# Two transformer blocks in split float32: seven held chunks with operand quarters between them, later head steps, and feed-forward pairs on one three-bank tag

## The chip, the cores and the metric

The kernel runs on one core of one Trainium2 chip. What is measured is the time of one execution on the device, in microseconds (us). A run of the program takes about 1.9 ms. The engines that matter are TensorE (PE in the profile; its weight loads are PEld), VectorE (DVE), ScalarE (ACT), GpSimd (POOL) and SyncE (SP), which issues the DMAs. PE writes its results to PSUM, which has eight banks of 512 float32 columns per partition.

## The reference

Two transformer blocks run one after the other on 256 tokens of width 2048, all in float32.

```python
# block 1
h = rms_norm(x, norm_g); proj = h @ w_in                      # 2048 -> 8192
ya = stick_breaking_attention(qa, ka, va); yb = chunk_band_attention(qb, kb, vb, ...)
x = x + concat(ya * silu(ga), yb * silu(gb)) @ w_out
# block 2
mod = silu(c) @ w_ada + b_ada                                 # 2048 -> 12288, six vectors
h = rms_norm_2(x, g_pre_mix) * (1 + sc1) + sh1; z = h @ w_in
o_a = mla_branch(cq, ckv, kr, ...)     # 16 heads, causal softmax
o_b = swa_branch(qs, ks, vs, ...)      # 32 heads of 64, window 128, a sink per head
mix = (sigmoid(za) * o_a + sigmoid(zb) * o_b) @ w_o
x = x + gt1 * rms_norm_2(mix, g_post_mix)
h = rms_norm_2(x, g_pre_ffn) * (1 + sc2) + sh2
u = causal_dwconv(h @ w_up)                                   # 2048 -> 2 x 5632, width 3
y = (silu(u[:, :5632]) * u[:, 5632:]) @ w_down
x = x + gt2 * rms_norm_2(y, g_post_ffn)
```

The 256 tokens are two token blocks of 128, which are called block 0 and block 1 of tokens below.

## The kernel before, in words

**Products.** A float32 product is made of three passes with each operand split into a high and a low part: `hi*hi + hi*lo + lo*hi`. In the projections the weight is stationary and the 256 tokens stream (256 columns, L270 to L272); in `wide` the first two passes share one matmul of 512 columns (L277) and the third has 256 (L278). Where an output row per token is wanted (`xmm`), 128 tokens are stationary and 256 or 512 weight columns stream (L293 to L295).

**The stream of weights.** `Stream` brings all weights in chunks of 128 x 1024 floats (512 KB): SP issues the DMA into one of five raw buffers, ACT writes the high part (`whi`, L123), DVE the low part (`wlo`, L125), and PE uses the two parts in the order in which the chunks were listed. Split chunks wait in slots. There are four (`AHEAD` is 3), and nine where a chunk was listed with `S.more` set (`AHEAD + 1 + MORE`). A slot is free when PE has used the chunk for the last time. Where PE keeps chunks for a second use, `S.base` stops the count, so that held chunks take slots which the chunks ahead would else have. `S.gate` puts a split behind a named instruction on ACT and DVE.

**Heads.** A head is a generator that the stream moves on by ticks, two for each chunk, which is 24 matmuls. Its softmax does DVE work on the scores, waits `DL[0]` ticks, does the exponentials on ACT, waits `DL[1]`, normalizes on POOL (`e`, L443, behind a reciprocal on DVE, L439), waits `DL[2]`, puts three transposes on PE (`t`, L450) which ACT copies to `pT`, waits `DL[3]`, and then `attend` puts three matmuls on PE (`o`, L457, L458). `DS` is the table of the 32 window heads, `DM` that of the 16 latent heads. On PE and SP instructions run in the order in which the code makes them; on ACT, DVE and POOL a scheduler orders them.

**The output projection and its end.** `mix @ w_o` goes in four column groups of 512, c = 0 to 3, of eight chunks each (`x_group`). Group 3 (tag `s`) handles the two token blocks apart: block 0 of tokens in every chunk, block 1 of tokens for the last `HOLD` = 4 chunks only after all of block 0. So `o_last(0)`, which closes block 0 of tokens (norm, residual `xs`, norm again, diagonal `dg`), runs beside the held matmuls. `operand(b, q)` makes a quarter of the feed-forward operand of token block b: four products with the diagonal on PE (`t`, L1390), scale and shift into `ht` on ACT and DVE, high part `h` on ACT, low part on DVE (L1400). `first_up` runs the first eight feed-forward chunks, again block 0 of tokens first (12 matmuls a chunk), with further `operand` calls between, then block 1 of tokens. `turn` brings its results over and starts the convolutions.

**Feed-forward pairs.** `up_pair(i)` fills two PSUM banks of two chunks each, the first of tag `g` (three banks) and the second of tag `s` (two); `post` reads a bank with ACT (`z`), DVE (L1556) and the convolution `conv` (L1511, L1513).

## Time and profile before

| | |
|---|---|
| median of three runs | 1911.71 us (1911.47 to 1912.13) |
| profiled execution | 1911.32 us |
| its span in the trace | 1909.5 us |
| PE busy | 1886.9 us (99%) |
| PEld, DVE, ACT, POOL busy | 1708.7, 1361.9, 1015.8, 193.0 us |
| chain of waits | PE 93%, DVE 2%, ACT 2%, issue 1%, DMA 1%, POOL 1% |
| HBM read | 434.73 MB, 229 GB/s over the span |

Busy times are sums over an engine's instructions; PE's ends are modelled. The span is what the trace covers, and the 1.8 us between it and the execution's time lie outside of it. PEclk in the profile is the share of full speed that TensorE's clock was granted. An instruction's idle time stands in brackets behind it with what ended it.

### The profile page before, as it was taken

Reading aid. Unit: us, or ns where it says so; the run is one execution under the profiler, and the core shown is the slowest. Engines: PE = TensorE matmul, PEld = TensorE weight load, DVE = VectorE, ACT = ScalarE, POOL = GpSimd, SP = SyncE. Lnnn points to the kernel's source line nnn. Section 1 sums busy time; section 2 is a strip of 40 time slices with the busy share of each in tenths; the row PEclk is TensorE's granted clock in tenths of the full one; section 3 lists DMA queues with packets and bytes.
Section 4 is the critical chain, followed back from the end, with each engine's and each line's share of the span. In section 5 each row is a group of like instructions: output and inputs, shape, how many; then the busy total and the mean of one; then the engine's idle time right before and its main releaser. Section 6 shows DMA issues by size and latency. Waiting matters only on the chain.

```text
span 1909.5 us, 31900 instructions
## 1 busy us (share of the span) xinstructions
PE 1886.9 (99%) x12148; PEld 1708.7 (89%) x12148; DVE 1361.9 (71%) x2211; ACT 1015.8 (53%) x1642; POOL 193.0 (10%) x298
## 2 busy tenths in 40 slices
PE   9999999999999999999999999999999999999998
PEld 9988889999999999999998878888888888888886
DVE  7777867767787777777877765888888777644444
ACT  7445454445555555554666556555555555543442
POOL 0001020001223323330123000000000000000000
PEclk9999999999999999999999999999999999999999
DMA  9888777757597877768655764777777665656564
GB/s 366 297 285 293 243 269 258 239 188 250 194 327 239 268 259 264 258 215 268 195 167 189 232 210 142 244 236 247 241 246 242 189 187 188 187 181 188 189 191 124
DMA packets 128169, 438.92 MB, mean 230 GB/s; under 512 B 14352, under 2 KB 20368, under 8 KB 127760
## 3 DMA queue, kind: packets, MB, share of 16 engines
q1 hardware_dynamic: 127872, 436.88, 69.6%
q8 instruction: 95, 1.56, 0.3%
q14 instruction: 58, 0.48, 0.1%
q10 hardware_dynamic: 144, 0.01, 0.0%
HBM read 434.73 MB, written 2.10 MB: 229 GB/s over the span
## 4 chain that ended last, share of the span: by engine, by line
PE 93%; DVE 2%; ACT 2%; issue 1%; DMA 1%; POOL 1%; SPq 0%; DVEq 0%; POOLq 0%; ACTq 0%
PE g L270 11%; PE g L271 11%; PE g L272 11%; PE s L277 8%; PE g L277 8%; PE g L293 7%; PE g L295 7%; PE g L294 7%; PE s L278 4%; PE g L278 4%; PE s L293 3%; PE s L294 3%; PE s L295 3%; PE o L457 1%; PE t L450 1%
## 5 line engine op out<-in xcount | busy, mean ns | idle before, releaser
L125 DVE TENSOR_TENSOR wlo<-raw,whi 128x1024 fp32r<-128x1024 f32 (+2 forms) x623 | 764.2, 1228 | 394.4 <-ACT whi L123 390.4
L123 ACT ACTIVATE whi<-raw 128x1024 fp32r<-128x1024 f32 (+2 forms) x623 | 652.0, 1048 | 631.5 <-PE g L271 136.8
L270 PE MATMUL g<-h,whi 128*128 128x256 f32 x880 | 253.6, 288 | 0.0
L272 PE MATMUL g<-h,wlo 128*128 128x256 f32 x880 | 247.8, 282 | 0.0
L271 PE MATMUL g<-h,whi 128*128 128x256 f32 x880 | 247.7, 281 | 0.0
L277 PE MATMUL s<-h,whi 128*128 128x512 f32 x672 | 240.7, 399 | 3.8 <-DVE u L1513 3.8
L392 DVE SCALAR_TENSOR_TENSOR raw<-raw,crep 128x1024 f32<-128x1024 f32 x192 | 240.7, 1254 | 2.1 <-DMA raw<-in_ada_dram 1.7
L277 PE MATMUL g<-h,whi 128*128 128x512 f32 x672 | 239.2, 397 | 0.0
L278 PE MATMUL s<-h,wlo 128*128 128x256 f32 x672 | 189.9, 283 | 0.0
L278 PE MATMUL g<-h,wlo 128*128 128x256 f32 x672 | 189.1, 281 | 0.0
L271 PEld LDWEIGHTS g<-h,whi 128*128 128x128 f32 x880 | 166.6, 189 | 0.0
L270 PEld LDWEIGHTS g<-h,whi 128*128 128x128 f32 x880 | 166.6, 189 | 0.0
L272 PEld LDWEIGHTS g<-h,wlo 128*128 128x128 f32 x880 | 166.3, 189 | 0.0
L277 PEld LDWEIGHTS s<-h,whi 128*128 128x128 f32 x672 | 126.9, 189 | 35.5 <-issue 4.0
L277 PEld LDWEIGHTS g<-h,whi 128*128 128x128 f32 x672 | 126.1, 188 | 31.1
L270 PE MATMUL g<-hx,whi 128*128 128x256 f32 x448 | 127.7, 285 | 0.0
L278 PEld LDWEIGHTS s<-h,wlo 128*128 128x128 f32 x672 | 127.4, 190 | 0.0
L278 PEld LDWEIGHTS g<-h,wlo 128*128 128x128 f32 x672 | 126.7, 188 | 0.0
L272 PE MATMUL g<-hx,wlo 128*128 128x256 f32 x448 | 125.8, 281 | 0.0
L271 PE MATMUL g<-hx,whi 128*128 128x256 f32 x448 | 125.8, 281 | 0.0
L293 PE MATMUL g<-whi,hx 128*128 128x512 f32 x256 | 104.6, 409 | 0.0
L295 PE MATMUL g<-whi,hx 128*128 128x512 f32 x256 | 101.0, 395 | 0.0
(351 smaller groups left out, 3872.3 us busy)
## 6 DMA issues: line engine op xcount, KB each, us to landing
raw<-in_ada_dram SPq DMA_DIRECT2D x192, 512.0 KB, 4.3
raw<-in_wup_dram SPq DMA_DIRECT2D x176, 512.0 KB, 4.3
raw<-in_w_dram SPq DMA_DIRECT2D x127, 512.0 KB, 4.8
raw<-in_wz_dram SPq DMA_DIRECT2D x122, 512.0 KB, 4.6
raw<-in_wdn_dram SPq DMA_DIRECT2D x88, 512.0 KB, 3.5
raw<-in_wo_dram SPq DMA_DIRECT2D x64, 512.0 KB, 4.4
raw<-in_wuq_dram SPq DMA_DIRECT2D x24, 384.0 KB, 3.5
raw<-in_wuv_dram SPq DMA_DIRECT2D x8, 512.0 KB, 4.5
```

The costliest lines, as they stand in the source:

```text
L123: nc.scalar.activation(out=hi[:, :n], in_=raw, func=AF.Copy)
L125: last = nc.vector.tensor_tensor(out=lo[:, :n], in0=raw, in1=hi[:, :n].bitcast(F32), op=ALU.subtract)
L270: mm(out, lhsT=whi, rhs=ahi, start=first, stop=False)
L271: mm(out, lhsT=whi, rhs=alo, start=False, stop=False)
L272: mm(out, lhsT=wlo, rhs=ahi, start=False, stop=last)
L277: mm(two(out), lhsT=whi, rhs=both, start=first, stop=False)
L278: mm(out[:, :T], lhsT=wlo, rhs=ahi, start=False, stop=last)
L293: mm(out, lhsT=ahi[:, t], rhs=hi[:, w], start=first, stop=False)
L294: mm(out, lhsT=ahi[:, t], rhs=lo[:, w], start=False, stop=False)
L295: mm(out, lhsT=alo[:, t], rhs=hi[:, w], start=False, stop=last)
L392: stt(out=raw, in0=raw, scalar=1.0, in1=crep_now[0][:, h * 1024:(h + 1) * 1024], op0=ALU.mult, op1=ALU.mult, accum_out=modh[:, k:k + 1])
L450: nc.tensor.transpose(pt[:, j * P:(j + 1) * P], e[:, j * P:(j + 1) * P], ident)
```

## The change

Four edits, with a constant or a list each for the first two.

- **The first window head** (h = 0) has its own table `DS0`, in which the transposes come two ticks later.
- **The latent heads** get `DM = (2,1,3,3)` instead of `(2,1,2,2)`: transposes one tick later, `attend` one more. Two more chunks of `o_second` stand before the chunk with `o_start`, which ends the last heads.
- **The end of the output projection** holds seven chunks instead of four. `mid` puts the operand quarters (0,0) and (0,1) behind the fifth of the seven held chunks; the four idle matmuls (`WARM`) go. `o_last(1)` makes residual and diagonal of token block 1 itself. `operand` works in two halves of two tiles, so that a quarter's high and low part are two instructions each. Operand (1,2) moves ahead of `out_z`, (1,3) to behind the second block.
- **Feed-forward pairs** take both of their banks from tag `g`.

```diff
-COLD, WARM = 24, 4
+COLD = 24
-    DS = (2,2,2,3)
-    DM = (2,1,2,2)
+    DS0, DS = (2,2,4,3), (2,2,2,3)
+    DM = (2,1,3,3)
...
-    def x_group(srcs, acts, handler, tot, width, tag="g", apart=None, listed=True):
+    def x_group(srcs, acts, handler, tot, width, tag="g", apart=None, listed=True, hold=HOLD, mid=None):
...
-                if apart is not None and c >= nch - HOLD:
+                if apart is not None and c >= nch - hold:
                     S.base = 1 << 30 if c == nch - 1 else min(S.base, S.nrun)
...
                 if c == nch - 1:
                     r.append(lambda: apart(0, box["b"][0]))
-                    r += [lambda j=j, d=d: one(box[d], d, j, 1) for d in range(c - HOLD + 1, c + 1) for j in js]
+                    for n, d in enumerate(range(c - hold + 1, c + 1)):
+                        if mid is not None and n == mid[0]:
+                            r += mid[1]
+                        r += [lambda j=j, d=d: one(box[d], d, j, 1) for j in js]
...
-        yield from softmax(sc, bias[:, 128:256], bias, pa, res, sink=h, eb=2, at=T, DL=DS)
+        yield from softmax(sc, bias[:, 128:256], bias, pa, res, sink=h, eb=2, at=T, DL=DS0 if h == 0 else DS)
...
         else:
-            idle = bank("o")
-            for _ in range(WARM):
-                mm(idle[:, :T], lhsT=mix[0][0][:, 0:P], rhs=mix[0][0], start=True, stop=True)
+            for c in range(4):
+                residual(b, c)
+            diagonal(b)
...
-            t = po.tile([P, 4, P], F32, tag="ht", name="ht", bufs=2)
...
+            last = None
             hi, lo = (hq[q][:, :, i, b * P:(b + 1) * P] for i in range(2))
-            return act(out=hi, in_=t, func=AF.Copy), tt(out=lo, in0=t, in1=hi.bitcast(F32), op=ALU.subtract)
...
+            for j in (0, 2):
+                t = po.tile([P, 2, P], F32, tag="ht%d" % j, name="ht", bufs=2)
+                for i in range(2):
+                    k = 4 * q + j + i
+                    src, g, h = ps[:, (j + i) * P:(j + i + 1) * P], ns["gs"][:, k:k + 1], mod[:, 48 + k:49 + k]
+                    if q < 2 and j == 2:
+                        ts(out=t[:, i], in0=src, scalar1=g, scalar2=h, op0=ALU.mult, op1=ALU.add)
+                    else:
+                        act(out=t[:, i], in_=src, func=AF.Identity, scale=g, bias=h)
+                last = (act(out=hi[:, j:j + 2], in_=t, func=AF.Copy),
+                        tt(out=lo[:, j:j + 2], in0=t, in1=hi[:, j:j + 2].bitcast(F32), op=ALU.subtract))
+            return last
...
+    def first_operands():
+        operand(0, 0)
+        S.gate = operand(0, 1)
+        parts()
...
-    for args in o_first[:7] + o_second[:2] + o_first[7:] + o_second[2:]:
+    for args in o_first[:7] + o_second[:4] + o_first[7:] + o_second[4:]:
...
-                apart=o_last if c == 3 else None)
+                apart=o_last if c == 3 else None, hold=7, mid=(5, [first_operands]))
...
-                if n != 1:
+                if n > 0:
                     S.gate = None, None
...
-                if n == 0:
-                    return first(0) + first(1) + [parts] + block(0, 0)
...
                 if n == 7:
-                    r += [lambda: out_z(0, 0), lambda: out_z(1, 0)]
+                    r += op(1, 2) + [lambda: out_z(0, 0), lambda: out_z(1, 0)]
                     for k in range(8):
                         r += block(k, 1)
-                        if k == 1 or k == 3:
-                            r += op(1, 2 + k // 2)
+                        if k == 1:
+                            r += op(1, 3)
...
             def pre(a=a):
-                box[a] = bank("gs"[a])
+                box[a] = bank("g")
```

How the instructions move is shown at three places, each before and then after.

On PE, the three transposes of the first window head (`t_6327<-cs0_69,e_6196` before, `t_6370` after; `g_6216` is the projection that runs beside it, `whi_6163` and `whi_6217` two following chunks of it). Before:

```order
L270 MATMUL g_6216<-h_5543,whi_6163 128x256
L271 MATMUL g_6216<-h_5544,whi_6163 128x256
L272 MATMUL g_6216<-h_5543,wlo_6164 128x256
L450 MATMUL t_6327<-cs0_69,e_6196 128x128 [waits PE_49,Pool_49]
L450 MATMUL t_6327<-cs0_69,e_6196 128x128 [waits Pool_49]
L450 MATMUL t_6327<-cs0_69,e_6196 128x128
L270 MATMUL g_6216<-h_5563,whi_6163 128x256
```

After, the place of the transposes is further down, behind 24 projection matmuls and four transposes of another task (`t_6343`), of which the last rows are:

```order
L270 MATMUL g_6216<-h_5589,whi_6163 128x256
L271 MATMUL g_6216<-h_5590,whi_6163 128x256
L272 MATMUL g_6216<-h_5589,wlo_6164 128x256
L1033 MATMUL t_6343<-cs0_69,xs_4199 128x128 [waits PE_49]
L1033 MATMUL t_6343<-cs0_69,xs_4199 128x128 x3
L270 MATMUL g_6216<-h_5609,whi_6217 128x256 [waits Activation_49]
...
L272 MATMUL g_6216<-h_5635,wlo_6218 128x256
L450 MATMUL t_6370<-cs0_69,e_6196 128x128 [waits PE_49,Pool_49]
```

The wait for POOL's `e_6196` is the same; it stands 28 PE instructions later in the program, past the first use of the chunk `whi_6217`.

On PE, the end of the output projection: `s_13280` is its last bank (token block 1), `t` are products with the diagonal, `g_13441` and `g_13471` the first feed-forward bank. Before:

```order
L295 MATMUL s_13280<-whi_13247,mix_12698 128x512
L1358 MATMUL o_13436<-mix_11451 128x256 x4
L1390 MATMUL t_13444<-dg2_13403,xs_4199 128x128 [waits DVE_49,PE_49]
L1390 MATMUL t_13444<-dg2_13403,xs_4199 128x128 x3
L1390 MATMUL t_13461<-dg2_13403,xs_4199 128x128 [waits PE_49]
L1390 MATMUL t_13461<-dg2_13403,xs_4199 128x128 x3
L293 MATMUL g_13441<-whi_13281,h_13443 128x256 [waits Activation_49]
L294 MATMUL g_13441<-wlo_13282,h_13443 128x256
L295 MATMUL g_13441<-whi_13281,h_13443 128x256 [waits DVE_49]
```

After:

```order
L295 MATMUL s_13280<-whi_13211,mix_12309 128x512
L1394 MATMUL t_13404<-dg2_13371,xs_4199 128x128 [waits DVE_49,PE_49]
L1394 MATMUL t_13404<-dg2_13371,xs_4199 128x128 x3
L1394 MATMUL t_13420<-dg2_13371,xs_4199 128x128 [waits PE_49]
L1394 MATMUL t_13420<-dg2_13371,xs_4199 128x128 x3
L293 MATMUL s_13280<-whi_13229,mix_12718 128x512
...
L295 MATMUL s_13280<-whi_13247,mix_12718 128x512
L293 MATMUL g_13471<-whi_13281,h_13403 128x256 [waits Activation_49]
L294 MATMUL g_13471<-wlo_13282,h_13403 128x256
L295 MATMUL g_13471<-whi_13281,h_13403 128x256 [waits DVE_49]
```

The operand's two groups of transposes now have the last two held chunks (12 matmuls) behind them, and the idle matmuls are gone.

On ACT, the splits of the first feed-forward chunks around `o_last` (`sq ... <-s_13279` is the first instruction of `o_last(0)`, `sq ... <-s_13280` of `o_last(1)`, `h` an operand's high part). Before:

```order
L123 ACTIVATE whi_13281<-raw_13179 128x1024 [waits DMAHW6_49,DVE_49]
L123 ACTIVATE whi_13299<-raw_13197 128x1024 [waits DMAHW7_49,DVE_49,PE_49]
L123 ACTIVATE whi_13317<-raw_13215 128x1024 [waits DMAHW0_49,DVE_49,PE_49]
L123 ACTIVATE whi_13335<-raw_13233 128x1024 [waits DMAHW1_49,DVE_49,PE_49]
L123 ACTIVATE whi_13351<-raw_13251 128x1024 [waits DMAHW2_49,DVE_49,PE_49]
L259 ACTIVATE sq_13381,ss_12901<-s_13279 128x512 [waits PE_49,Activation_49]
```

After:

```order
L123 ACTIVATE whi_13281<-raw_13179 128x1024 [waits DMAHW6_49,DVE_49]
L123 ACTIVATE whi_13299<-raw_13197 128x1024 [waits DMAHW7_49,DVE_49,PE_49]
L259 ACTIVATE sq_13349,ss_12940<-s_13279 128x512 [waits PE_49,Activation_49]
...
L259 ACTIVATE h_13419<-ht_13430 128x2x128 [waits DVE_49]
L123 ACTIVATE whi_13487<-raw_13215 128x1024 [waits DMAHW0_49]
L259 ACTIVATE sq_13447,ss_12940<-s_13280 128x512 [waits PE_49]
L123 ACTIVATE whi_13493<-raw_13233 128x1024 [waits DMAHW1_49]
L259 ACTIVATE rv_13449<-ss_12940 128x1 [waits Activation_49]
L123 ACTIVATE whi_13497<-raw_13251 128x1024 [waits DMAHW2_49]
```

Two feed-forward chunks are split ahead of `o_last(0)` instead of five; the next three (`raw_13215`, `raw_13233`, `raw_13251`) come behind the two operand quarters, among the work of `o_last(1)`. SP issues DMAs of the same kinds in the same sequence in both kernels; among the chunks of `w_o`, two of group 1 are brought before the last one of group 0.

## Rows read from the trace of the kernel before

**Rows 1.** The page: busy time, share of the span and instructions of PE, granted clock.

```profile
PE 1886.9 (99%) x12148; PEld 1708.7 (89%) x12148; DVE 1361.9 (71%) x2211; ACT 1015.8 (53%) x1642; POOL 193.0 (10%) x298
...
PEclk9999999999999999999999999999999999999999
```

**Rows 2.** What PE waited for: us in total, times, longest us.

```profile
PE s L277 <- DVE u L1513: 3.8, 1, 3.8
PE t L450 <- POOL e L443: 3.5, 4, 2.3
PE o L457 <- ACT pT L259: 2.0, 4, 1.0
PE g L293 <- ACT h L259: 1.5, 1, 1.5
```

**Rows 3.** Windows: length, busy time of five engines, granted clock, DMA share, GB/s.

```profile
564.00:568.00 4.00, 2.53 (x14) 2.34 (x15) 4.00 (x10) 1.68 (x6) 2.72 (x4) 0.81 0.96 365
568.00:572.00 4.00, 4.00 (x29) 4.00 (x29) 2.57 (x3) 1.61 (x2) 3.85 (x7) 0.77 0.80 284
...
1144.00:1148.00 4.00, 4.00 (x37) 4.00 (x36) 4.00 (x8) 4.00 (x6) 0.00 (x0) 1.00 0.00 0
...
1184.00:1188.00 4.00, 4.00 (x16) 3.37 (x15) 2.48 (x5) 2.18 (x4) 0.00 (x0) 0.57 0.13 22
```

**Rows 4.** Timeline, PE, first window head (start, duration, instruction, [idle before]).

```profile
562.60 0.28 PE L272 MATMUL g<-h,wlo 128*128 128x256 f32 x1
565.23 0.33 PE L450 MATMUL t<-cs,e 128*128 128x128 f32 x1 [2.35 <-POOL e L443]
565.80 0.44 PE L450 MATMUL t<-cs,e 128*128 128x128 f32 x2 [0.24 <-POOL e L443]
```

**Rows 5.** Timeline, POOL: the two normalizing steps of a window and a latent head.

```profile
564.77 0.97 POOL L443 TENSOR_TENSOR e<-e,st 128x128 f32<-128x128 f32 x2 [2.38 <-DVE st L439]
...
1043.46 1.95 POOL L443 TENSOR_TENSOR e<-e,st 128x128 f32<-128x128 f32 x2 [5.32 <-PE o L458]
```

**Rows 6.** Timeline, PE, from block 1's held matmuls to the first pair.

```profile
1132.65 0.40 PE L293 MATMUL s<-whi,mix 128*128 128x512 f32 x1
...
1138.25 0.63 PE L1358 MATMUL o<-mix 128*128 128x256 f32 x4
...
1142.88 0.38 PE L293 MATMUL g<-whi,h 128*128 128x256 f32 x1 [1.49 <-ACT h L259]
...
1146.35 1.05 PE L1390 MATMUL t<-dg,xs 128*128 128x128 f32 x8
1147.15 0.36 PE L293 MATMUL g<-whi,h 128*128 128x256 f32 x1
...
1150.04 1.05 PE L1390 MATMUL t<-dg,xs 128*128 128x128 f32 x8
...
1172.99 0.39 PE L277 MATMUL g<-h,whi 128*128 128x512 f32 x1
```

**Rows 7.** Timeline, DVE: the diagonal of token block 0.

```profile
1138.93 0.29 DVE L1379 TENSOR_SCALAR dg<-cs,rv 128x128 f32<-128x128 f32 x1 [1.16 <-ACT rv L259]
```

**Rows 8.** Groups by line and shape, ACT and DVE: count, busy us, mean ns, idle.

```profile
L123 ACT ACTIVATE whi<-raw 128x1024 fp32r<-128x1024 f32 x597 | 630.6, 1058 | 621.1 <-PE g L271 133.7 <-PE g L295 127.2 <-issue 106.6
...
L125 DVE TENSOR_TENSOR wlo<-raw,whi 128x1024 fp32r<-128x1024 f32 x597 | 738.5, 1238 | 391.5 <-ACT whi L123 387.6 <-DMA raw<-in_ada_dram 1.2 <-DMA raw<-in_wz_dram 1.1
L1521 DVE TENSOR_TENSOR u<-u 128x256 f32<-128x256 f32 x44 | 18.4, 419 | 0.1
L1365 DVE SCALAR_TENSOR_TENSOR xs<-y,rv,xs 128x512 f32<-128x512 f32 x8 | 5.6, 747 | 0.0
L1400 DVE TENSOR_TENSOR h<-ht,h 128x512 fp32r<-128x512 f32 x8 | 5.5, 689 | 4.2 <-ACT h L259 4.2
```

**Rows 9.** Timeline, PE, between the two banks of the first pair.

```profile
1179.30 0.28 PE L278 MATMUL g<-h,wlo 128*128 128x256 f32 x1
1183.34 0.47 PE L277 MATMUL s<-h,whi 128*128 128x512 f32 x1 [3.76 <-DVE u L1513]
```

More of the change, by code (lines that the diff above doesn't have):

```diff
@@ L565, in fs @@
                 js = range(per)
-                if apart is not None and c >= nch - HOLD:
+                if apart is not None and c >= nch - hold:
                     S.base = 1 << 30 if c == nch - 1 else min(S.base, S.nrun)
-                if apart is None or c < nch - HOLD:
+                if apart is None or c < nch - hold:
                     return [lambda j=j, b=b: one(w, c, j, b) for j in js for b in range(2)]
@@ L1338, in o_handler @@
         return h
-    hq = []
+    hq, hf_ = [], []
     def o_last(b, ps):
@@ L1390, in operand, with parts @@
                 mm(ps[:, j * P:(j + 1) * P], lhsT=xs[:, k, b * P:(b + 1) * P], rhs=ns["dg", b], start=True, stop=True)
-            t = po.tile([P, 4, P], F32, tag="ht", name="ht", bufs=2)
-            for j in range(4):
-                k = 4 * q + j
-                g, h = ns["gs"][:, k:k + 1], mod[:, 48 + k:49 + k]
-                if q < 2 and j > 1:
-                    ts(out=t[:, j], in0=ps[:, j * P:(j + 1) * P], scalar1=g, scalar2=h, op0=ALU.mult, op1=ALU.add)
-                else:
-                    act(out=t[:, j], in_=ps[:, j * P:(j + 1) * P], func=AF.Identity, scale=g, bias=h)
-            hi, lo = (hq[q][:, :, i, b * P:(b + 1) * P] for i in range(2))
-            return act(out=hi, in_=t, func=AF.Copy), tt(out=lo, in0=t, in1=hi.bitcast(F32), op=ALU.subtract)
-    def first_operand(q):
-        hi, lo = operand(0, q)
-        if q == 1:
-            S.gate = hi, lo
-        if q < 2:
-            residual(1, 2 * q, lo)
-            residual(1, 2 * q + 1, lo)
-        if q == 1:
-            diagonal(1, lo)
+            last = None
+            hi, lo = (hq[q][:, :, i, b * P:(b + 1) * P] for i in range(2))
+            for j in (0, 2):
[10 more added lines that the diff above has]
+            return last
+    def parts():
+        for h in hq[len(hf_) // 4:]:
+            hf_.extend((h[:, j, 0], h[:, j, 1], h[:, j]) for j in range(4))
+    def first_operands():
+        operand(0, 0)
+        S.gate = operand(0, 1)
+        parts()
     o_first = x_group(lambda k: wo2[k], lambda: mix, o_handler(0), 16, 512, tag="g", listed=False)
@@ L1420, in two_blocks @@
         x_group(lambda k, c=c: wo2[8 * c + k], lambda: mix, o_handler(c), 16, 512, tag="gs"[c % 2],
-                apart=o_last if c == 3 else None)
-    hf_ = []
+                apart=o_last if c == 3 else None, hold=7, mid=(5, [first_operands]))
     def first_up():
@@ L1444, in fs @@
                 S.base = 1 << 30 if n == 7 else min(S.base, S.nrun)
-                if n != 1:
+                if n > 0:
                     S.gate = None, None
                 op = lambda b, q: [lambda: operand(b, q)]
-                first = lambda q: [lambda: first_operand(q)]
-                if n == 0:
-                    return first(0) + first(1) + [parts] + block(0, 0)
                 r = block(n, 0)
                 if n == 1 or n == 3:
-                    r += first(2 + n // 2) + [parts]
+                    r += op(0, 2 + n // 2) + [parts]
                 if n == 5 or n == 6:
@@ L1464, in mms @@
             return fs
-        def parts():
-            for h in hq[len(hf_) // 4:]:
-                hf_.extend((h[:, j, 0], h[:, j, 1], h[:, j]) for j in range(4))
         def pre(n):
```

## The prediction, on record before the changed kernel ran

> **What bounds the kernel now.** I read the page first. PE is busy for 1886.9 of 1909.5 us, and the granted clock is nine tenths or more in every slice [rows 1], so the change can only win back the 22.6 us in which PE stands still, and what a lowered clock adds behind a stop. Next comes the list of what PE waited for [rows 2]: one wait of 3.8 us for DVE's `u`, four of 3.5 us in all for POOL's `e`, four of 2.0 us for `pT`, one of 1.5 us for `h`. Each belongs to a place that one of the four edits touches. Windows around these places come third: the clock was 0.81 and 0.77 behind the longest `e` wait and 0.57 behind the `u` wait, but 1.00 just behind the wait for `h` [rows 3]. So two of the stops cost more than they last. Last, timelines at each place tell what is late next.
>
> The sums are made against the profiled execution, 1911.32 us (span 1909.5 and 1.8 outside). The median of the runs is 1911.71, so 0.39 is added at the end.
>
> **First window head.** PE has issued its last projection matmul by 562.60 + 0.12 = 562.72 and then waits 2.35 and 0.24 us for `e` [rows 4]; behind it, two windows of 4 us at 0.81 and 0.77 of full speed lose 0.76 + 0.92 [rows 3]. Together 4.3 us. The change puts 24 matmuls and four transposes ahead of the wait. Twenty-four such matmuls take 2.89 us, from 1147.15 to 1150.04, and eight transposes of this size 0.80 [rows 6], so PE arrives at 562.72 + 2.89 + 0.40 = 566.0. POOL ends `e` at 564.77 + 0.97 = 565.74 [rows 5]; nothing is put before it on DVE or POOL. The stop goes with 0.3 us to spare. What is late next: the chunk that PE then reaches early was split on DVE before `e` was made, and the following heads have their tables unchanged. No DMA hangs on the step. I take -4.3; the bounds are 0 (the stop moves on whole to the next split) and -4.5.
>
> What of those 0.3 us? In this head two steps of `e` took 0.97 us, in a latent head 1.95 [rows 5], though both are of one shape. The Trainium skill (SBUF — State Buffer, Who interferes with whom) says that a VectorE instruction with two SBUF inputs, as the low part of a split is, contends with a GpSimd instruction that reads SBUF. The two rows agree that `e` has no fixed length. By the rows' worse case PE would wait 566.7 - 566.0 = 0.7 us here, which makes -3.6; as the instructions around this `e` stay the same, I keep 0.97.
>
> **Latent heads.** All waits for `e` and `pT` but the 2.59 of the first head are theirs: 3.5 + 2.0 - 2.6 = 2.9 us in six stops, the longest 1.0 [rows 2]. One tick is 24 matmuls, so the transposes come 1.4 us or more later in PE's order against a wait of at most 0.65, and `attend` two ticks later against one of 1.0. Added waits: none; the scores' bank and `pT` have two buffers each, and a head now spans two more ticks. Two more `w_o` chunks stand before the last heads' end, so these are further from it; on SP only the order among `w_o` chunks moves. One of the late heads stays near: its `e` ends at 1043.46 + 1.95 = 1045.4 [rows 5], and PE would now arrive within 0.3 us of that. I take -2.6; bounds -2.9 and 0, where each stop reappears at the later place.
>
> **End of the output projection.** Let zero be the end of token block 0 in group 3. Before, that is 1132.65; the 24 held matmuls last until 1138.25 (0.233 each), and pair work starts at 1172.99 [rows 6]: 40.3 us. After, 18 more matmuls (4.2 us) lie behind zero, so the same work costs 44.5 us by the old way. Without any wait it is 42 x 0.233 = 9.8 for the held matmuls, 16 blocks of twelve at 2.89 / 2 = 1.445, 23.1, and eight quarters of transposes at 0.80, 6.4: 39.3. At most 5.2 us can be had.
>
> First, the diagonal is ready at 1138.93 + 0.29 [rows 7], 6.57 after zero. Thirty held matmuls take 7.0, so PE comes to the transposes 0.4 late, where it waited before; the last twelve held matmuls (2.8) cover the making of `h`, for which PE stood 1.5 us at 1142.88 [rows 2, 6]. That part works; were the diagonal late, the twelve held matmuls queued behind it would wait with it, and what they cover would show again.
>
> Against it stands the shortage of slots. Seven of nine are held, so two feed-forward chunks are split ahead and not five. Three splits more, 1.06 on ACT and 1.24 on DVE each [rows 8], fall into the stretch in which before already had DVE and ACT busy for 4.00 of 4.00 us [rows 3]. I follow DVE from operand (0,1), done 10.6 after zero (PE leaves the transposes at 8.6, then 2.0 for scale, shift and split): five splits, 6.2; `xs` four times 0.75 and `y` 0.7, 3.7; low parts of three quarters in halves, 6 x 0.42, 2.5; scale and shift of one quarter and small steps, 1.5. That is 13.9, so the split for the seventh chunk is ready at 24.5 if DVE never rests, and I add 0.7 for ACT, whose three splits stand before operand (0,2): 25.2. PE without waits would come there at 7.0 + 1.6 + 2.8 + 6 x 1.445 + 3 x 0.8 = 22.5. So it waits 2.7, and the part saves 5.2 - 2.7 = 2.5. Half quarters are in this sum: one low part of 0.69 becomes two of 0.42 [rows 8], 0.15 us more each. Bounds: -5.2 where splits are in time, +0.2 where the waits are twice as long.
>
> **Pairs on three banks.** Between the halves of the first pair PE stops from 1179.30 to 1183.34, 3.76 of it for `u`, since the two `s` banks still hold what `turn` made [rows 9]. Then a window at 0.57 loses 0.43 x 4 = 1.7 [rows 3]. Together 5.5. A third `g` bank was emptied before the first pair began, so the second half starts at once. Next late would be a split: ACT still does the transition's steps in the same order, and by the rows' durations the second chunk of the next pair is split 1.2 us before PE comes, the fourth 0.3 before. I take -5.4; bounds -5.5, and -2 if such a split comes 1 or 2 us late and the clock falls again.
>
> **Sum.** -4.3 - 2.6 - 2.5 - 5.4 = -14.8 on 1911.32: 1896.5, and 1896.9 against the median.
>
> **Rivals.**
> - *Splits in time.* ACT and DVE rested for much of the run (53% and 71% busy [rows 1]), and the scheduler may place the late splits better than my sum. Then C's 5.2 and the latent heads' 2.9 come whole: 1911.7 - 4.3 - 2.9 - 5.2 - 5.5 = 1893.8. Against it: that stretch alone is full.
> - *The end of the projection gives nothing.* Waits of 5.4 us before the fifth and seventh chunk: 1911.7 - 4.3 - 2.6 + 0.2 - 5.4 = 1899.6, and with the clock lowered once, as in the 0.77 and 0.81 windows, 1901.3. For it: ACT and DVE both full; against: PE is halted twice, not once for long.
> - *A stop only moves.* The first head's or the first pair's stop reappears at the next split, so that one of 4.3 and 5.4 is lost: 1901.2 or 1902.3. The small margins, 0.3 in each, speak for it; that the engines in question idle while PE waits speaks against it.
> - *The change doesn't do what it says.* PE halts at the moved places just as long, and three of four parts give nothing: within 0.2% (3.8 us, about what these runs can tell from no change) of 1911.7.
> - *Three banks are too few (slower).* All 84 halves of the 42 pairs now go through three banks, and a bank must be empty two halves, 11.2 us (1172.99 to 1179.42 is one half with 0.8 of transposes [rows 6, 9]), after it was filled. From the point where `z` is later than that, every half waits; at 0.3 us each, 83 halves cost 24.9, 10.1 more than the rest saves: 1921.8. The list of waits speaks against it: no half but one waited for a bank [rows 2], and there the bank held something else. The Trainium skill (TensorE: Matmul & The Clock Gate, A second HAM failure mode: psum-queue depth-cycling) tells of a kernel that cycled through PSUM banks, idled a little between groups, and had its clock go down and up. By it the half-empty waits would cost more than they last. Here the clock was nine tenths or more in every slice of these halves [rows 1], so the trace does not bear it out.
>
> **How the numbers follow.** Forecast 0.50 (its own range 1895 to 1899); splits in time 0.18; projection's end gives nothing 0.13; a stop only moves 0.09; no effect 0.06; slower 0.04. The first four are faster by over 0.2%: 0.90; same 0.06; slower 0.04. A range from 1892 to 1903.5 holds the first four but for their tails, some 0.85.
>
> **What would show it.** In the trace after: no wait for `e` near 565 and a granted clock of 1.00 there; the list's `t <- e` and `o <- pT` rows under 0.7 us; PE at the diagonal's products without a wait; waits for low parts or `h` before the fifth and seventh feed-forward chunk, 2.7 us in all; no wait between the halves of the first pair. Wrong would be waits for `g` banks in the pairs, a clock below 1.00 around the eight feed-forward chunks, or a new long row in the list of waits.

## The result and the profile after

The changed kernel takes 1886.52 us (median of four runs, 1885.87 to 1888.16), the kernel before 1911.84 beside it (1911.47 to 1912.13). The ratio is 0.9877 [0.9856, 0.9898]: 25.3 us less. The forecast was 14.8 less. The direction was right, and so was each of the four edits' own; the time lies 5.5 us below the range.

The profiled execution took 1886.98 us, with a span of 1885.2. The page after, busy time, which answers [rows 1]:

```profile
PE 1873.0 (99%) x12144; PEld 1704.0 (90%) x12144; DVE 1360.2 (72%) x2219; ACT 1015.4 (54%) x1650; POOL 188.6 (10%) x298
```

PE's idle time went from 22.6 to 12.2 us, 10.4 less. But its busy time fell too, by 13.9 us, with four matmuls fewer out of 12148. Some 3.4 of that is the lowered clock of [rows 3]; the other 10 us are, but for those four, the same instructions in less time, and no wait that is gone. That is the first sign of what the prediction missed.

What PE waited for after, all rows from 0.3 us up, which answers [rows 2]:

```profile
PE t L811 <- DVE zero L808: 1.2, 1, 1.2
PE s L270 <- ACT whi L123: 0.9, 1, 0.9
PE t L450 <- POOL e L443: 0.8, 1, 0.8
PE s L272 <- DVE wlo L125: 0.8, 1, 0.8
PE g L294 <- DVE wlo L125: 0.3, 1, 0.3
PE g L295 <- DVE h L1407: 0.3, 1, 0.3
```

The waits for `u` and `pT` are gone and one of `e` is left. No row names a bank.

Windows after at the first window head and between the halves of the first pair (length, busy time of PE, PEld, DVE, ACT, POOL, granted clock, DMA share, GB/s), which answer [rows 3]:

```profile
564.00:568.00 4.00, 4.00 (x36) 4.00 (x36) 4.00 (x10) 2.23 (x7) 1.93 (x4) 1.00 0.92 283
568.00:572.00 4.00, 4.00 (x36) 4.00 (x35) 3.82 (x9) 2.32 (x5) 3.93 (x5) 1.00 0.97 332
...
1168.00:1172.00 4.00, 4.00 (x25) 3.54 (x24) 1.99 (x6) 2.58 (x5) 0.00 (x0) 1.00 0.92 378
```

The clock stays at 1.00 where it was 0.81, 0.77 and 0.57.

PE's timeline after, at the places of the four edits, which answers [rows 4, 6, 9]:

```profile
567.57 0.49 PE L450 MATMUL t<-cs,e 128*128 128x128 f32 x3
...
1041.86 0.44 PE L450 MATMUL t<-cs,e 128*128 128x128 f32 x2 [0.77 <-POOL e L443]
...
1128.82 1.95 PE L1394 MATMUL t<-dg,xs 128*128 128x128 f32 x16
...
1142.80 0.38 PE L295 MATMUL g<-whi,h 128*128 128x256 f32 x1 [0.26 <-DVE h L1407]
...
1146.21 0.39 PE L294 MATMUL g<-wlo,h 128*128 128x256 f32 x1 [0.27 <-DVE wlo L125]
...
1162.98 0.40 PE L277 MATMUL g<-h,whi 128*128 128x512 f32 x1
...
1169.41 0.39 PE L277 MATMUL g<-h,whi 128*128 128x512 f32 x1
```

The first head's transposes (567.57), the diagonal's products (1128.82) and the second half of the first pair (1169.41) start without a wait. To see where time was won, I set each matmul of the two traces beside its counterpart and took the difference of their starts, after less before. It stays level where the two run alike and falls where the changed kernel gains:

| stretch (times of after) | difference, from and to | gain |
|---|---|---|
| start, to 16 us | 0 to +1.64 | -1.64 |
| first window head, 560 to 576 | +1.64 to -3.00 | 4.64 |
| latent heads, 911 to 1082 | -3.00 to -6.64 | 3.64 |
| end of the projection, 1121 to 1163 | -6.64 to -10.01 | 3.37 |
| between the halves of the first pair | -10.01 to -15.60 | 5.59 |
| the rest of the pairs, to 1630 | -15.60 to -24.37 | 8.77 |
| down projection, to the end | -24.37 to -24.36 | 0.0 |

The start is no part of the change: over the other profiles, with the same code there, it lies between -0.2 and +3.6 against before. The row that nobody counted is the one before the last: 8.77 us, spread evenly over the pairs, with no wait in them.

There a step is one matmul of 512 columns (L277) and the one of 256 (L278) behind it. The L277 of PE's timeline in the pairs, one to a step, of before and then of after:

```profile
1199.78 0.39 PE L277 MATMUL s<-h,whi 128*128 128x512 f32 x1
...
1200.12 0.40 PE L277 MATMUL s<-h,whi 128*128 128x512 f32 x1
...
1200.48 0.39 PE L277 MATMUL s<-h,whi 128*128 128x512 f32 x1
...
1200.83 0.40 PE L277 MATMUL s<-h,whi 128*128 128x512 f32 x1
...
1201.19 0.39 PE L277 MATMUL s<-h,whi 128*128 128x512 f32 x1
```

```profile
1199.92 0.39 PE L277 MATMUL g<-h,whi 128*128 128x512 f32 x1
...
1200.26 0.39 PE L277 MATMUL g<-h,whi 128*128 128x512 f32 x1
...
1200.61 0.39 PE L277 MATMUL g<-h,whi 128*128 128x512 f32 x1
...
1200.96 0.39 PE L277 MATMUL g<-h,whi 128*128 128x512 f32 x1
...
1201.30 0.39 PE L277 MATMUL g<-h,whi 128*128 128x512 f32 x1
```

Four steps take 1.41 us before and 1.38 after. Before, every second step is longer: they take 0.346 and 0.361 us by turns. Averaged over hundreds of steps, a step is 0.3533 us before and 0.3467 after; 0.0067 times the 1320 or so steps of that row is 8.8, which is all of it. The same shows in the durations of L277 (count, min/median/max ns, first and last start, forms). Before, for 1199 to 1300, then after, for 1200 to 1380:

```profile
L277 PE MATMUL g<-h,whi x144: 392/397/402, 1201.9 to 1297.6; 128*128 128x512 f32 x144
L277 PE MATMUL s<-h,whi x143: 392/402/402, 1198.7 to 1299.8; 128*128 128x512 f32 x143
```

```profile
L277 PE MATMUL g<-h,whi x520: 392/392/392, 1199.9 to 1379.8; 128*128 128x512 f32 x174
```

After, every one takes 392 ns; before, 392 and 402 by turns, in both tags. The same view of before, for the last eight steps ahead of its 3.76 us stop:

```profile
L277 PE MATMUL g<-h,whi x8: 392/392/480, 1176.6 to 1179.1; 128*128 128x512 f32 x8
```

But for the first of them, which follows transposes, they take 392 ns, as after. So before had the lower step too, and lost it at the stop.

### The profile page after: what moved, and what is told of

Same layout as the page of the kernel before. It is cut to its first block, busy times and chain, and to the rows that moved or that the text cites. A ratio compares the mean times of both kernels' runs of the same rounds, so it can differ in the third digit from the quotient of the medians.

```text
span 1885.2 us, 31970 instructions
## 1 busy us (share of the span) xinstructions
PE 1873.0 (99%) x12144; PEld 1704.0 (90%) x12144; DVE 1360.2 (72%) x2219; ACT 1015.4 (54%) x1650; POOL 188.6 (10%) x298
## 4 chain that ended last, share of the span: by engine, by line
PE 97%; ACT 1%; DVE 1%; DMA 0%; POOL 0%; issue 0%; SPq 0%; DVEq 0%; POOLq 0%
PE g L277 16%; PE g L270 12%; PE g L272 12%; PE g L271 12%; PE g L278 8%; PE g L294 7%; PE g L295 7%; PE g L293 7%; PE s L293 3%; PE s L294 3%; PE s L295 3%; PE o L457 1%; PE t L450 1%; PE s L1132 1%; PE o L458 1%; PE s L272 1%
## 5 line engine op out<-in xcount | busy, mean ns | idle before, releaser
L277 PE MATMUL g<-h,whi 128*128 128x512 f32 x1344 | 466.1, 392 | 0.0
L278 PE MATMUL g<-h,wlo 128*128 128x256 f32 x1344 | 376.3, 280 | 0.0
L277 PEld LDWEIGHTS g<-h,whi 128*128 128x128 f32 x1344 | 252.3, 188 | 56.4
L278 PEld LDWEIGHTS g<-h,wlo 128*128 128x128 f32 x1344 | 252.7, 188 | 0.0
L272 PE MATMUL g<-h,wlo 128*128 128x256 f32 x880 | 247.2, 281 | 0.0
L271 PEld LDWEIGHTS g<-h,whi 128*128 128x128 f32 x880 | 166.0, 189 | 0.0
L270 PEld LDWEIGHTS g<-h,whi 128*128 128x128 f32 x880 | 166.0, 189 | 0.0
L272 PEld LDWEIGHTS g<-h,wlo 128*128 128x128 f32 x880 | 165.8, 188 | 0.0
L294 PE MATMUL g<-wlo,hx 128*128 128x512 f32 x256 | 101.0, 395 | 0.0
L270 PEld LDWEIGHTS g<-hx,whi 128*128 128x128 f32 x448 | 84.5, 189 | 0.1
L271 PEld LDWEIGHTS g<-hx,whi 128*128 128x128 f32 x448 | 84.5, 189 | 0.1
L272 PEld LDWEIGHTS g<-hx,wlo 128*128 128x128 f32 x448 | 84.4, 188 | 0.0
```

The source lines that it names most:

```text
L270: mm(out, lhsT=whi, rhs=ahi, start=first, stop=False)
L271: mm(out, lhsT=whi, rhs=alo, start=False, stop=False)
L272: mm(out, lhsT=wlo, rhs=ahi, start=False, stop=last)
L277: mm(two(out), lhsT=whi, rhs=both, start=first, stop=False)
L278: mm(out[:, :T], lhsT=wlo, rhs=ahi, start=False, stop=last)
L294: mm(out, lhsT=ahi[:, t], rhs=lo[:, w], start=False, stop=False)
```

## The experiments

The question was what sets the step: the third bank, the stop, the clock that falls behind it, or something else. On the way the first three edits were undone one at a time. Below, "step" is the mean over a hundred steps or more. In all profiles it took one of two values, 0.3467 or 0.3533. The 0.3527 in an expectation below is the 0.3533 taken over the 15 steps within one half, eight of them short and seven long. Each ratio is against runs of the kernel before on the same chip.

**Only the first pair's stop taken away** (on the kernel before).

```diff
-                box[a] = bank("gs"[a])
+                box[a] = bank("g" if i == 2 else "gs"[a])
```

> The kernel before, with tag g for both banks of the first feed-forward pair alone; the other 41 pairs alternate g and s as before. In the two traces, one 512- and one 256-column matmul of a pair together took 0.3527 us in all pairs behind the stop of the kernel before, and 0.3467 in the changed kernel. Theory stop (a stop of PE with a lowered clock leaves the slower rate behind it, whatever the banks): no stop in the first pair, 0.347 in all pairs, 5.5 + 8.8 us less than before, 1897.5. Theory banks (the slower rate belongs to halves that alternate between the tags): the stop's 5.5 us go, 0.353 stays from the second pair on, 1906.3. Theory chance or another edit: 1906.3 as well, at 0.353 from the first pair on.

Measured: 1897.61 us, ratio 0.9954 [0.9934, 0.9974]; the step is 0.3467 in the halves of tag `g` and of tag `s` alike:

```profile
L277 PE MATMUL s<-h,whi x261: 392/392/392, 1201.1 to 1380.0; 128*128 128x512 f32 x131
L277 PE MATMUL g<-h,whi x260: 392/392/392, 1199.7 to 1378.2; 128*128 128x512 f32 x130
```

With one bank moved in one pair the profiled execution (1896.47) has the lower step in all 42. The theory that the tag sets it falls. The seven executions lie in two groups, 1894.8 to 1897.6 (four) and 1904.0 to 1905.4 (three): without the stop the longer time is rarer than in the kernel before, but not gone.

**Only the three banks undone** (on the changed kernel).

```diff
-                box[a] = bank("g")
+                box[a] = bank("gs"[a])
```

> The changed kernel, with the fourth edit undone (the second bank of each pair is of tag s again). Theories stop and banks: the stop of about 3.8 us before the second half of the first pair is back with the lowered clock behind it, and pairs at 0.353: 1886.5 + 5.6 + 8.8 = 1900.9. Theory that the faster rate comes from one of the other three edits: the stop is back, pairs at 0.347: 1892.1.

Measured: 1900.82 us, 0.9959 [0.9945, 0.9974]. The wait and the window behind it are back:

```profile
PE s L277 <- DVE u L1511: 3.8, 1, 3.8
```

```profile
1172.00:1176.00 4.00, 4.00 (x15) 3.40 (x16) 2.65 (x6) 2.17 (x4) 0.00 (x0) 0.59 0.16 23
```

The step is 0.3533 from there on. This edit alone is worth some 14 us (1900.82 against the changed kernel's 1886.5), 5.6 for the stop and the rest for the step.

**Alternating tags in all pairs but the first** (on the changed kernel).

```diff
-                box[a] = bank("g")
+                box[a] = bank("g" if i == 2 else "gs"[a])
```

> The changed kernel with tags g and s alternating again in all pairs but the first, so that nothing stops before or in the pairs. What the first four runs showed: a stop with a lowered clock was followed by pairs at 0.353 in three profiles of three, without one they went at 0.347 on either tags; and executions of one kernel with such stops fell into two groups some 8 us apart. Theory stop, as it stands now (the rate of the pairs is drawn anew, fast or slow, when the clock comes back, and is kept until the next time): one group, all fast, 0.347, 1886.5 within 2. Theory banks: 0.353 in 41 of 42 pairs, 1895.

Measured: 1885.77 us, 0.9877 [0.9859, 0.9894], step 0.3467 throughout. So the third bank is needed in the first pair only.

**A stop put before pair 22**, by a small matmul that waits for a chain of subtractions on POOL: six in the first kernel, one in the second (the `range(6)` is `range(1)`).

```diff
...
+                if i == 22 and c == 0:
+                    mm(bank("o")[:, 0:P], lhsT=late[0][:, 0:P], rhs=late[0][:, 0:P], start=True, stop=True)
...
+                if i == 21 and a == 1:
+                    d = ns["pf"].tile([P, T], F32, tag="late", name="late", bufs=1)
+                    late.append(d)
+                    for r in range(6):
+                        nc.gpsimd.tensor_tensor(out=d, in0=d if r else z, in1=z, op=ALU.subtract)
```

> The changed kernel with a stop put into the middle of the pairs: before pair 22 one small matmul waits for a chain of six subtractions on POOL, which is idle there. PE should stand still for 4 to 6 us, and the clock should fall for one window as it did behind the stop of the kernel before. Theory stop: 0.347 before pair 22, 0.353 behind it to the end of the pairs, 22 pairs of 32 steps at 0.006 more = 4.2 us beside the stop's own 5 to 7.5: 1895.7 to 1898.2. Theory banks: 0.347 on both sides, 1891.5 to 1894.

> The same with one subtraction, so that PE stands still for about 1.5 us and the clock should stay at full speed. If any stop sets the slower rate: 0.353 behind pair 22, 1886.5 + 1.5 + 4.2 = 1892.2. If it takes the lowered clock: 0.347 on both sides, 1888.0. Theory banks: 1888.0.

Measured: the first stopped for 8.6 us, with the clock at 0.52 and 0.50, and took 1901.9 us, 0.9971 [0.9952, 0.9989]. The second, meant to be short, stopped for 4.3, with the clock at 0.70 and 0.87, and took 1896.51, 0.9938 [0.9919, 0.9958]. In both the step is 0.3467 up to the stop and 0.3533 behind it. So the higher step can begin in the middle of the pairs, and it is not the turn between the stages. But both had the clock down, and both put a matmul in.

**A stop without a lowered clock**: the matmul waits for ACT's copy of a bank just finished.

```diff
...
+                if i == 22 and c == 0:
+                    mm(bank("o")[:, 0:P], lhsT=late[0], rhs=late[0], start=True, stop=True)
...
+                if i == 21 and a == 1:
+                    late.append(ns["pf"].tile([P, P], F32, tag="late", name="late", bufs=1))
+                    act(out=late[0], in_=box[a][:, :P], func=AF.Copy)
```

> The changed kernel with a stop of 1 to 2 us before pair 22: one small matmul waits for ACT's copy of the bank that was just finished. The earlier try at a short stop lasted 4.3 us and lowered the clock. Theory that the rate is drawn by the lowered clock: clock at 1.00, 0.347 on both sides, 1886.5 + 1.5 = 1888.0 in one group. Theory that any stop draws it: 0.353 behind it in part of the executions, up to 1892.2.

Measured: 1893.39 us, 0.9910 [0.9892, 0.9928]. The stop in the timeline of PE, the window that holds it, and L277 in a stretch ahead of it and one behind it:

```profile
1389.10 0.49 PE L1548 MATMUL o<-late 128*128 128x128 f32 x2 [1.24 <-ACT late L259]
```

```profile
1388.00:1392.00 4.00, 2.90 (x17) 2.57 (x18) 3.32 (x6) 2.23 (x5) 0.00 (x0) 1.00 0.77 214
```

```profile
L277 PE MATMUL g<-h,whi x520: 392/392/392, 1199.8 to 1379.7; 128*128 128x512 f32 x174
...
L277 PE MATMUL g<-h,whi x567: 392/392/402, 1399.7 to 1599.7; 128*128 128x512 f32 x189
```

The granted clock is 1.00 and the step still goes from 0.3467 to 0.3533. A lowered clock is not needed for it.

**The same matmul without anything to wait for**, and then **an extra matmul of the pairs' own form** in its place:

```diff
+                if i == 22 and c == 0:
+                    mm(bank("o")[:, 0:P], lhsT=ident, rhs=ident, start=True, stop=True)
```

```diff
+                if i == 22 and c == 0:
+                    mm(bank("o"), lhsT=hf_[0][0][:, 0:P], rhs=hf_[0][2], start=True, stop=True)
```

> A control for the runs with a stop before pair 22: the changed kernel with the same small matmul there, but reading a constant, so that PE waits for nothing. If a stop draws the rate of the pairs: 0.347 on both sides, 1886.5 + 0.1. If the foreign matmul itself disturbs the stream: 0.353 behind it, 1890.7.

> The control with a matmul of the pairs' own kind: one more 512-column matmul in the split format before pair 22, no wait. If the foreign float32 matmul of the control disturbed by its form (it is run as two instructions): 0.347 on both sides, 1886.8. If any further step in the alternation of 512 and 256 columns does it: 0.353 behind it, 1890.9.

Measured: 1891.7 us, 0.9907 [0.9881, 0.9932], and 1892.9, 0.9916 [0.9891, 0.9942]. The timeline of the first, and its L277 ahead of and behind it:

```profile
1386.11 0.39 PE L1548 MATMUL o<-cs 128*128 128x128 f32 x2
1386.25 0.49 PE L277 MATMUL g<-h,whi 128*128 128x512 f32 x1
```

```profile
L277 PE MATMUL g<-h,whi x520: 392/392/392, 1200.0 to 1379.9; 128*128 128x512 f32 x174
...
L277 PE MATMUL g<-h,whi x567: 392/402/402, 1399.8 to 1599.7; 128*128 128x512 f32 x189
```

There is no idle time, and the step behind it is 0.3533, as it is behind the extra 512-column matmul. This was to be the control in which nothing happens, and it took the theory of the stop with it: one matmul too many at that place is enough, without any wait. The runs with a stop before pair 22 all put such a matmul in, so they do not show what a wait does by itself. A wait with no matmul added, at which the step rises, stands only in the first pair of the kernel before and of the run with the three banks undone, and there the clock fell too. On the 704 steps behind the added matmul 0.0067 us makes 4.7, against 5.3 between 1891.7 and the 1886.4 of the changed kernel's repeat below.

**Five short stops**, before pairs 8, 14, 20, 26 and 32 (the edit of the stop without a lowered clock, at five places).

```diff
+    STOPS = (8, 14, 20, 26, 32)
...
+                if i in STOPS and c == 0:
+                    mm(bank("o")[:, 0:P], lhsT=late[-1], rhs=late[-1], start=True, stop=True)
...
```

> The changed kernel with five short stops, before pairs 8, 14, 20, 26 and 32, each a small matmul that waits for ACT's copy of the bank just finished (1.2 us in the run with one). Theory that each stop draws the rate anew: stretches of six pairs at 0.347 and at 0.353 in one profile, with changes in both directions, and executions that differ by up to 36 x 32 x 0.006 = 6.9 us. Theory that a stop always leads to the slow rate, or that it stays slow once it is: 0.347 up to pair 8, 0.353 from there on; 1886.5 + 5 x 1.4 + 6.9 = 1900.4 in all executions.

Measured: 1902.92 us, 0.9963 [0.9953, 0.9974]. L277 ahead of the first stop, behind the first and behind the fifth:

```profile
L277 PE MATMUL g<-h,whi x117: 392/392/392, 1179.8 to 1220.0; 128*128 128x512 f32 x117
...
L277 PE MATMUL g<-h,whi x142: 392/397/402, 1239.9 to 1289.7; 128*128 128x512 f32 x142
...
L277 PE MATMUL g<-h,whi x227: 392/392/402, 1519.9 to 1599.7; 128*128 128x512 f32 x114
```

The step is 0.3467 up to the first stop and 0.3533 in each of the five stretches behind it. None of the later stops brought the lower one back; all that differs between the stretches is which of two neighbouring steps is the long one.

**The first head's edit undone.**

```diff
-        yield from softmax(sc, bias[:, 128:256], bias, pa, res, sink=h, eb=2, at=T, DL=DS0 if h == 0 else DS)
+        yield from softmax(sc, bias[:, 128:256], bias, pa, res, sink=h, eb=2, at=T, DL=DS)
```

> The changed kernel with the first edit undone (the first window head has table DS). The stop of 2.6 us at the first head is back with its lowered clock: 4.6 us by the traces, 1891.1. Theory that the rate of the pairs is drawn when the clock comes back and then kept for the rest: two groups of executions, 1891 and 1899, since the draw is now at 570. If the draw only holds for the stretch in which it is made: one group, 1891.1, 0.347 in the pairs.

Measured: 1889.52 us, 0.9893 [0.9878, 0.9909], and 2.1 us more than the changed kernel by the matmuls set side by side, not the 4.6 expected. The stop is back, but shorter than in [rows 4], and behind it the clock does not fall:

```profile
564.72 0.33 PE L450 MATMUL t<-cs,e 128*128 128x128 f32 x1 [1.34 <-POOL e L443]
565.29 0.44 PE L450 MATMUL t<-cs,e 128*128 128x128 f32 x2 [0.24 <-POOL e L443]
```

```profile
564.00:568.00 4.00, 3.04 (x24) 2.85 (x25) 3.54 (x10) 2.56 (x7) 3.15 (x5) 1.00 0.99 333
```

In the first experiment above, on the kernel before, too, this wait was 1.48 and 0.24 us at a clock of 1.00. When POOL comes to `e` varies by some 1 us against PE between executions; the 4.3 of the forecast was the price in one of them.

**The latent heads' edit undone.**

```diff
-    DM = (2,1,3,3)
+    DM = (2,1,2,2)
...
-    for args in o_first[:7] + o_second[:4] + o_first[7:] + o_second[4:]:
+    for args in o_first[:7] + o_second[:2] + o_first[7:] + o_second[2:]:
```

> The changed kernel with the second edit undone (DM and the place of o_start as before). The traces give that part 3.6 us (2.9 in waits, the rest in what follows each wait): 1890.1. The six stops are short and 100 us ahead of the pairs, where the last edits leave only two of 0.3 us: pairs at 0.347 in all executions, if the rate is drawn at the last stop before them.

Measured: 1893.52 us (executions of 1889.2, 1893.2, 1893.8 and 1898.1), 0.9915 [0.9891, 0.9939]. The four waits for `pT` are back with 2.0 us, and the matmuls fall 3.7 us behind those of the changed kernel, 1.5 of it before 1033 us; the pairs keep 0.3467 in the profiled execution (1889.18).

**The end of the projection undone**: four held chunks, whole operand quarters, the idle matmuls.

```diff
-                apart=o_last if c == 3 else None, hold=7, mid=(5, [first_operands]))
+                apart=o_last if c == 3 else None)
...
-            for c in range(4):
-                residual(b, c)
-            diagonal(b)
+            idle = bank("o")
+            for _ in range(WARM):
+                mm(idle[:, :T], lhsT=mix[0][0][:, 0:P], rhs=mix[0][0], start=True, stop=True)
```

> The changed kernel with the third edit undone (four held chunks, quarters behind them, WARM, as before). The traces give that part 3.4 us (from 44.5 to 41.2 between the end of token block 0 and the first pair): 1889.9. Theory that only a lowered clock draws the rate: its stops are short (1.5 us at most) and the clock stays up, so one group of executions, pairs at 0.347. Theory that any stop of PE draws it: two groups, 1889.9 and 1898.

Measured: 1898.83 us, 0.9935 [0.9913, 0.9956], but in executions of 1891.8 (one) and of 1898.6 to 1900.8 (three). In the profiled one (1891.84, step 0.3467) the stretch costs 4.2 us more than in the changed kernel, and the old wait is there:

```profile
1136.88 0.38 PE L293 MATMUL g<-whi,h 128*128 128x256 f32 x1 [1.49 <-ACT h L259]
```

Of the three longer executions here, and of the three with the latent heads' edit undone, no trace was kept; they lie 4 to 9 us above the profiled ones, and what makes that difference is not shown.

**One more slot for split chunks**, alone, and with another tick for the latent heads (`DM = (2,1,4,3)`).

```diff
-    RAW, AHEAD, MORE = (5,3,5)
+    RAW, AHEAD, MORE = (5,3,6)
```

> The changed kernel with one more wide slot (MORE 6) and nothing else: three feed-forward chunks split ahead of the end of the projection. The two waits of 0.3 us among the eight feed-forward chunks should go: 0.5 us less than the changed kernel in the same call, which is near what can be told; 0.347 in the pairs. If any disturbance ahead of the pairs draws the rate anew: some executions 8 us higher.

> A version meant to be faster than the changed kernel: one more wide slot (MORE 6, so that three feed-forward chunks are split ahead of the end of the projection instead of two) and DM = (2,1,4,3), since the one wait of 0.77 us that is left among the latent heads is for POOL's step. Expected: that wait gone, and of the 1.9 us that the eight feed-forward chunks still lose some 0.5: 1885.2, pairs at 0.347. If the later transposes make the heads late instead: 1887.

Measured: alone 1893.53 us, 0.9904 [0.9881, 0.9927], in executions of 1885.3 (two) and 1893.3 to 1896.0 (four). The profiled one is of the second group, and has the higher step from the first pair on, without a stop anywhere near:

```profile
L277 PE MATMUL g<-h,whi x510: 392/397/402, 1199.8 to 1379.7; 128*128 128x512 f32 x170
```

The wait for `wlo` at the eight chunks is gone, but 1885.3 against 1885.3 to 1888.2 of the changed kernel is no gain that can be told. With the later tick 1902.96, 0.9958 [0.9939, 0.9977]: the last heads end too late, and three waits for `qr` take 7.1 us; here too the step is 0.3533 from the first pair on.

**The changed kernel once more.**

> The changed kernel once more, unchanged, beside the kernel before on one chip. Its first four executions lay within 2.3 us. If nothing disturbs its pairs, all executions stay in one group near 1886.5 with 0.347 in the pairs, and those of the kernel before fall into groups near 1902 and 1910. If the rate is drawn in this kernel too, some executions lie 8 us higher.

Measured: 1886.36 us, 0.9887 [0.9866, 0.9908]; the executions are 1885.6 to 1888.8 (five) and 1896.85 (one). The profiled one, 1888.77, has 0.3467. No version that was tried beats the changed kernel by more than can be told; the one with alternating tags in 41 pairs equals it.

The groups of times fit the step. Of 57 executions of the kernel before that were timed beside these experiments, 9 took 1900.6 to 1902.6 us and 48 took 1908.9 to 1914.6; the 8 to 9 us between them are near the 8.8 of the longer step. The profile of the kernel before is of the upper group; that the lower step ran in those 9 is argued from the sum and not seen in a trace. On the changed kernel that stop is gone, and one of its ten executions (four beside the result, six here) lies in an upper group.

## Why the prediction was wrong

- **First window head** (-4.3, measured -4.64). Right in this pair of profiles: no wait, clock 1.00. `e` came 0.85 us earlier against PE than before, so the margin was 1.0 us and not 0.3. The experiment shows that the size is that of one execution, in which the clock fell behind the stop; set against the profile with the edit undone it gives 2.1. That the forecast of this part came out so close is in part luck.
- **The length of `e`.** POOL's timeline after, first window head and late latent head, which answers [rows 5]:

```profile
565.56 0.97 POOL L443 TENSOR_TENSOR e<-e,st 128x128 f32<-128x128 f32 x2 [2.38 <-DVE st L439]
...
1038.87 2.93 POOL L443 TENSOR_TENSOR e<-e,st 128x128 f32<-128x128 f32 x2 [7.93 <-DVE st L439]
```

The first kept 0.97, as taken. The late one went to 2.93, and PE waited 0.77 for it at 1041.86: the head that was said to "stay near", by more than the 0.3 allowed. That `e` has no fixed length agrees with the rule of the Trainium skill that was weighed there (SBUF — State Buffer, Who interferes with whom); no run here isolates the port.
- **Latent heads** (-2.6, measured -3.64; undone alone 3.7). Right in direction, sized too small. Of 2.9 us of waits 0.8 is left, so 2.1 of the gain is idle time. Most of the other 1.5 us is that a stop costs more than the idle time counted ahead of it. PE's timeline before, at the longest `pT` wait:

```profile
1041.03 0.39 PE L295 MATMUL g<-whi,mix 128*128 128x512 f32 x1
1042.38 0.70 PE L457 MATMUL o<-pT,v 128*128 128x256 f32 x2 [0.96 <-ACT pT L259]
...
1043.37 0.40 PE L294 MATMUL g<-wlo,mix 128*128 128x512 f32 x1
```

From the first to the last of these starts are 2.34 us; the same instructions without a wait take 1.13, from 1049.45 to 1050.58. So the stop cost 1.21 with an idle time of 0.96. Read in this way, the six stops cost 0.23 to 0.27 us each above their idle time, 4.4 in all, and the one that is left 1.0: 3.4 of the 3.64. (The prediction also has a tick as 24 matmuls; it is half a chunk, 12, and its 1.4 us are those of 12.)
- **End of the projection** (-2.5, measured -3.37; undone alone 4.2). The diagonal was ready at 1128.40, 0.42 ahead of PE, as worked out [rows 7]:

```profile
1128.11 0.29 DVE L1383 TENSOR_SCALAR dg<-cs,rv 128x128 f32<-128x128 f32 x1 [1.16 <-ACT rv L259]
```

The waits for splits and `h` were forecast at 2.7 us and are 0.53: the sum for DVE was too pessimistic, and the rival "splits in time" was right on that. The wait-free time in turn was too low, 39.3 against 41.2 - 0.5 = 40.7, so the two errors offset each other in part. The half low parts took the 0.42 us of the estimate [rows 8]:

```profile
L1407 DVE TENSOR_TENSOR h<-ht,h 128x256 fp32r<-128x256 f32 x16 | 6.6, 421 | 5.6 <-ACT h L259 5.4
```

- **Pairs on three banks** (-5.4). This is the step that failed. It says that a stop of 3.76 and a slow window cost "together 5.5", and these were worth 5.59. But it put the pace of the pairs behind the stop at no change, without a look at it; and the prediction's opening says that the change can win back only idle time and a lowered clock. With the stop gone the pairs keep 0.3467 us a step where they had 0.3533: 8.8 us more, none of it a wait. With this edit undone the stop and the 0.3533 are back together. The rows for it were in the trace of before, ahead of and behind the stop.
- **Three banks too few.** It did not come: no wait for a bank in 84 halves, clock 1.00. What the Trainium skill tells of a kernel that cycles through PSUM banks (TensorE: Matmul & The Clock Gate, A second HAM failure mode: psum-queue depth-cycling) did not show here: PE did not idle between the halves.

In sum: the four edits as forecast gave 17.2 against 14.8, and the missed term 8.8; the start took 1.6 back. With the missed term the forecast would have been 1888.1.

What stays open is what decides between the two steps. `turn`'s eight transposes break the stream some 3 us after the first pair begins, and in every profile the step behind them is the one ahead of them: 0.3467 in 15 profiles, 0.3533 in the two with one slot more. So not every break raises the step, and whether the number of matmuls put in counts no run tells. By their times, edits far ahead of the pairs (slots, held chunks, latent heads) change the share of executions in either group, so the 8.8 us are not the fourth edit's alone in every execution. What in PE makes every second 512-column matmul 10 ns longer was not found either.

## What to carry to other kernels

After finding a stop, measure the pace of the same instructions ahead of it and behind it, not only the stop and the clock: a few nanoseconds on some 1300 steps were worth more than the stop itself. A fall of PE's busy time at the same count of instructions says that the pace changed, and where the difference of matched starts falls evenly, no wait is the cause. In a long regular stream a stray instruction can cost far more than its own time, here 4.7 us for one matmul, and a kernel whose executions lie in two groups should be read in both before an edit is priced.

## What the runs showed of the hardware

- The same alternation of 512- and 256-column matmuls ran at 0.3467 or at 0.3533 us a step at a granted clock of 1.00, and at no third value. At the higher one every second step is longer, most of it in the 512-column matmul (402 against 392 ns). Either value held for hundreds of steps. It went up behind a wait of 3.76 us with a lowered clock, and behind one extra matmul without any wait; with one slot more it was up from the first pair on. In no profile did it go down, and eight transposes in the stream left it as it was.
- The stretches of one width, of 256 columns (16 to 560 and 576 to 911 us) and of 512 (the down projection), took the same time in both kernels.
- A stop among the latent heads cost PE 0.23 to 0.27 us above its idle time.
- The granted clock of a window was 0.81 and 0.77 behind a wait of 2.59 us, 0.57 behind 3.76 and 0.50, the lower of its two levels throughout, in a window of the 8.6 us stop. It was 1.00, the higher level, behind waits of 1.24, 1.58 and 1.72 us.
